# Reordering the vector engine's steps inside each attention unit of a hybrid encoder block: sums of q and the split of turned softmax weights first, scaling and block transposes of the next head behind them

## The chip, the cores and the metric

One Trainium2 chip, one core. The metric is device time in microseconds of one execution of the whole program (one encoder layer, batch 1, 256 positions, width 2048, everything float32 from and to HBM). The kernel before takes 915.23 us (median of three runs, 915.09 to 915.6).

## What is computed

One layer: RMSNorm, one input projection into q, k, v and u, windowed attention with ALiBi and a sink logit on q, k, v (12 query heads of 128, 4 key heads, so three query heads share a key head), a Fourier mix on u, an output projection with residual, then a convolutional gated feed-forward with residual, then a last RMSNorm. What the change touches is the attention:

```
scores = einsum('bnqkgd,bnskd->bnkgqs', qb, kb) * HEAD_DIM ** -0.5
scores = where(valid, scores + alibi, NEG_INF)
m = maximum(max(scores, axis=-1), sink_b)
p = exp(scores - m)
p = p / (sum(p, axis=-1) + exp(sink_b - m))
out = einsum('bnkgqs,bnskd->bnqkgd', p, vb)
...
x = x + concatenate([rmsnorm(out), fourier], -1) @ w_out
x = x + conv_ffn(rmsnorm(x)); return rmsnorm(x)
```

## The kernel before

Float32 accuracy is reached on TensorE with split operands: every operand is written as a high part `hi` (rounded by ScalarE, `nc.scalar.activation(hi, raw, AF.Copy)`, L185) and a low part `lo = raw - hi` (VectorE, L186), and a product is formed from hi x hi, lo x hi and hi x lo. So each weight tile that is streamed in (128 x 2048 floats, 1 MB) costs one long ScalarE instruction and one long VectorE instruction. In the profile PE is TensorE, DVE is VectorE, ACT is ScalarE, POOL is GpSimd and SP is the engine that issues most DMAs.

The first half of the program is a row of numbered **units**, one weight tile each. Units 4 to 7 make v, units 8 to 23 make the q and k heads in the order k0 q0 q1 q2, k1 q3 q4 q5, k2 q6 q7 q8, k3 q9 q10 q11, units 24 to 39 are the output projection. A unit is run by

```
def unit(i, work):
    run(before, i)
    work(*halves.pop(i))
    run(beside, i)
    step(i)
    run(behind, i)
```

`work` is the unit's matmuls (for a q or k head 32 of them, L395 and L397, about 5.25 us). `before` holds other matmuls that run first on TensorE; `beside` and `behind` hold the small steps of the other engines, and `step(i)` between them splits the weight tile of unit i + 2 (L185, L186) and then issues the load of the tile of unit i + 5 from SP. The order is written out by hand: each engine takes its instructions strictly in the order in which the program names them, and waits in place for whatever the next one needs.

A query head whose matmuls run in unit s goes through these steps afterwards:

- unit s + 1, `qk_out` (L637 ACT copies half of the PSUM result to `tmp`, L639 DVE adds the halves: the "sum of q") and `qk_parts` (L234 ACT, L235 DVE: the hi and lo of q, tile `qT`). A key head does the same with L639, L641, L654, L655.
- unit s + 2, `scores` (six matmuls, L665, in `before`, each lo part of q used by the third of each three), `scores_out` (DVE, L681 to L686) and, in `behind`, `exps` (ACT, L695 and L699).
- unit s + 3, `weigh` (DVE, L704 to L708: sum, reciprocal and scaling by it) and `turn` (L715: VectorE transposes blocks of 32 x 32 into the one buffer `tb`; L720: SP writes it to DRAM, tile `turn`).
- unit s + 4, `fetch` (L726: four DMAs from SP read the blocks back from DRAM in turned order into `td`, two buffers).
- unit s + 5, `turn_out` (L739 ACT, L740 DVE: hi and lo of the turned weights, tiles `pt`).
- unit s + 6, `values` (six matmuls, L768, in `before`; the second one already needs the lo part) and `values_out` (L492 and L234 on ACT, L235 on DVE, tile `cat`; a sum on POOL, L497).

The last head, 11, is transposed by TensorE instead (`turn_last`, `turn_last_out`, unit 27) and its values are formed in unit 28 with those of head 10.

Because every fourth unit is a key head, the duties of VectorE and ScalarE repeat with a period of four units. By what they hold, four kinds of unit are told apart below, named after an example in the middle:

- kind 18 (units 14, 18, 22): weigh, turn, sum and parts of a q, turn_out.
- kind 19 (15, 19, 23): sum and parts of a q, scores_out, values_out, turn_out.
- kind 20 (16, 20, 24): weigh, turn, sum and parts of a q, scores_out, values_out, turn_out.
- kind 21 (13, 17, 21, 25): weigh, turn, sum and parts of a k (in 25: none), scores_out, values_out; no turn_out.

All of them end with the split of a weight tile. The order in which a unit's small steps are queued is the order of the `at(beside, ...)` calls in the loop at L782 to L820, which is what the change edits. On DVE it is before: weigh, turn, sum of q, (k), parts, scores_out, values_out, turn_out, split. On SP a unit queues fetch, the write of turn, and, after the split has released its buffer, the load.

Of the kernel before, what the change touches and what calls it, by code (L numbers as in the profile page):

```python
# [96 lines left out]
def block_kernel(  # L97
# [42 lines left out]
    def bank(pool, name):  # L140
        return pool.tile([P, 512], F32, tag=pool.name, name=name)
# [63 lines left out]
    for n, size in enumerate(U_LOADS[1:], 1):  # L205
        k = sum(U_LOADS[:n])
# [18 lines left out]
    ps = bank(dn, "ps_warm")  # L225
# [68 lines left out]
    k = 0  # L294
# [119 lines left out]
    before, beside, behind = {}, {}, {}  # L414

    def at(when, i, f, *a):
        when.setdefault(i, []).append((f, a))
# [214 lines left out]
    qk_sb, st = {}, {}  # L632
    sq_a = ph.tile([P, S], F32, tag="sq", name="sq_a")

    def qk_out(kind, h, ps):
        tmp = ph.tile([P, S], F32, tag="tmp", name=f"tmp_{kind}{h}", bufs=2)
        nc.scalar.activation(tmp, ps[:, S : 2 * S], AF.Copy)  # L637
        add = ph.tile([P, S], F32, tag="add", name=f"add_{kind}{h}", bufs=2)
        nc.vector.tensor_tensor(add, ps[:, 0:S], tmp, ALU.add)  # L639
        if kind == "k":  # L640
            nc.vector.tensor_tensor(add, add, r1b, ALU.mult)  # L641
        st["add", kind, h] = add
# [139 lines left out]
    for i in range(N_QK, N_OUT + 8):  # L782
        heads = {i - s: h for (kind, h), s in slot_of.items() if kind == "q"}
        new = [kh for kh, s in slot_of.items() if i - s == 1]
        if i - 9 in range(NG):
            at(before, i, fourier_channels, i - 9)
        valued = [h for d, h in heads.items() if d == (5 if h == NH - 1 else 6)]
        for h in valued:
            at(before, i, values, h, mm if i < N_OUT else dn)
        turned = {d: h for d, h in heads.items() if h < NH - 1}  # L790
        last = {d: h for d, h in heads.items() if h == NH - 1}
        if 4 in last:
            at(before, i, turn_last, last[4])
        if i == 15:
            at(before, i, total, sq_f, "f")
        if 2 in heads:
            at(before, i, scores, heads[2])
        if 4 in turned:
            at(beside, i, fetch, turned[4])
        if 3 in heads:  # L800
            at(beside, i, weigh, heads[3])
        if 3 in turned:
            at(beside, i, turn, turned[3])

        for kind, h in new:
            if kind == "q":
                at(beside, i, lambda k=kind, h=h: qk_out(k, h, st.pop(("ps", k, h))))
        if 4 in last:
            at(beside, i, turn_last_out, last[4])
        for kind, h in new:  # L810
            if kind == "k":
                at(beside, i, lambda k=kind, h=h: qk_out(k, h, st.pop(("ps", k, h))))
            at(beside, i, qk_parts, kind, h)
        if 2 in heads:
            at(beside, i, scores_out, heads[2])
            at(behind, i, exps, heads[2])
        for h in valued:
            at(beside, i, values_out, h)
        if 5 in turned:
            at(beside, i, turn_out, turned[5])  # L820

    fourier_channels_steps()
    for n, (kind, h) in enumerate(QK_ORDER):
# [57 lines left out]
    for n, (c, kq) in enumerate(OUT_ORDER):  # L881
        i = N_OUT + n
# [14 lines left out]
        if kq >= 2:  # L897
            part = "a" if kq == 2 else "f"
            ps = ps_a[c] if kq < 3 else ps_a[c, "f"]
            last = c in added  # L900
# [306 lines left out]
    for q in range(2):  # L1207
        kind, j = items[q]
        ps = bank(mm, f"ps_{kind}{j}")
# [16 lines left out]
    for n, it in enumerate(items):  # L1226
# [8 lines left out]
        if it[0] in ("gate", "val"):  # L1235
            kind, j = it
            ps = bank(mm, f"ps_{kind}{j}")
# [4 lines left out]
        if it[0] == "product":  # L1242
            kind, g, c, p = it
# [3 lines left out]
            for cc in (0, 1) if both else (c,):  # L1247
# [5 lines left out]
                ps = bank(mm, f"ps_{p}{g}{cc}")  # L1253
# [6 lines left out]
        else:  # L1260
            kind, g, c = it
            hi, lo = halves.pop(up_index[n])
            ps = [bank(mm, f"ps_l{g}{c}{b}") for b in range(2)]
# [10 lines left out]
    i = up_index[n]  # L1274
# [156 lines left out]
```

## Time and profile before

| what | value |
| --- | --- |
| median of 3 runs | 915.23 us |
| the profiled execution, its own time | 915.61 us |
| its span, first to last instruction | 913.8 us, so 1.8 us lie around it |
| mean granted TensorE clock | 0.992 |
| PE busy over the span | 896.7 us (98%) |
| DVE busy | 753.5 us (82%) |
| ACT busy | 546.0 us (60%) |
| POOL busy | 53.2 us (6%) |
| DMA moved | 220.62 MB, 241 GB/s |

The profile's columns: a row of the timeline is start, duration (us), engine, line, operation, tiles (written <- read), shapes, count, and in brackets the idle time of the engine before it with what ended it. A row of the waits is who waited for whom: total us, times, longest. A row of the windows is the stretch, its length, then busy time and (x instructions) of PE, PE's weight loads, DVE, ACT and POOL, then the granted TensorE clock (1.00 is full speed), the DMA share and GB/s. Attention's units 12 to 28 lie between 75 and 190 us of the span.

### The profile page before, as it was taken

The numbers are of one execution on the slowest core, as the hardware profiler recorded it, in microseconds if no ns is written. First come the engines' busy times: TensorE is split into PE (matmuls) and PEld (weight loads), VectorE is DVE, ScalarE is ACT, GpSimd is POOL, SyncE is SP. The second block draws the span as 40 slices with busy tenths as digits, with TensorE's granted clock in tenths as the row PEclk, the third lists the DMA queues.
The fourth block names the chain that finished last, engine by engine and source line by source line (L and its number), as shares of the span: only waits on it lengthen the run. The fifth ranks groups of instructions, "written<-read, shape, count | busy, mean of one in ns | idle before, by whom it ended". The sixth has DMA issues, their size and how long they took to land.

```text
span 913.8 us, 12775 instructions
## 1 busy us (share of the span) xinstructions
PE 896.7 (98%) x5020; PEld 808.9 (89%) x5020; DVE 753.5 (82%) x905; ACT 546.0 (60%) x661; POOL 53.2 (6%) x65
## 2 busy tenths in 40 slices
PE   9999898999999999999999999999999999999996
PEld 7899787988899999999999999999999999999885
DVE  7668888867668787889888898878988789988996
ACT  7756556655545656556655575555665555656544
POOL 0001101010000000000000000000000000000004
PEclk9999899999999999999999999999999999999999
DMA  9964566655559687686988779896887987789752
GB/s 362 333 231 173 185 204 195 229 199 180 207 180 305 232 265 230 209 264 206 300 243 274 241 282 248 258 320 209 284 262 237 312 276 237 242 259 272 221 198 92
DMA packets 40827, 220.62 MB, mean 241 GB/s; under 512 B 4512, under 2 KB 10528, under 8 KB 16448
## 3 DMA queue, kind: packets, MB, share of 16 engines
q1 hardware_dynamic: 36512, 190.06, 56.2%
q0 software_dynamic: 4112, 29.49, 17.4%
q8 instruction: 39, 0.64, 0.3%
q10 hardware_dynamic: 144, 0.26, 0.1%
q14 instruction: 20, 0.16, 0.0%
HBM read 214.81 MB, written 4.98 MB: 241 GB/s over the span
## 4 chain that ended last, share of the span: by engine, by line
PE 83%; DVE 8%; ACT 4%; issue 2%; DMA 1%; POOL 1%; ACTq 0%; POOLq 0%; DVEq 0%
PE ps_val L395 16%; PE ps_gate L395 16%; PE ps_gate L397 8%; PE ps_val L397 8%; DVE parts L186 4%; PE ps_P L1148 3%; PE ps_P L1149 3%; PE ps_P L1150 3%; PE ps_N L1148 2%; PE ps_N L1150 2%; PE ps_N L1149 2%; PE ps_u L289 2%; PE ps_a L379 2%; PE ps_a L378 2%; PE ps_a L380 2%
## 5 line engine op out<-in xcount | busy, mean ns | idle before, releaser
L186 DVE TENSOR_TENSOR parts<-raw,parts 128x2048 fp32r<-128x2048 f32 (+1 forms) x129 | 293.2, 2273 | 49.9 <-ACT parts L185 47.1
L185 ACT ACTIVATE parts<-raw 128x2048 fp32r<-128x2048 f32 (+1 forms) x129 | 245.5, 1903 | 43.2 <-PE ps_a L380 12.4
L395 PE MATMUL ps_val<-hU,parts 128*128 128x512 f32 x688 | 227.7, 382 | 0.0
L395 PE MATMUL ps_gate<-hU,parts 128*128 128x512 f32 x688 | 227.3, 382 | 0.0
L397 PE MATMUL ps_val<-hU,parts 128*128 128x256 f32 x688 | 187.7, 273 | 0.0
L397 PE MATMUL ps_gate<-hU,parts 128*128 128x256 f32 x688 | 187.0, 273 | 0.0
L395 PEld LDWEIGHTS ps_val<-hU,parts 128*128 128x128 f32 x688 | 130.6, 190 | 17.7
L395 PEld LDWEIGHTS ps_gate<-hU,parts 128*128 128x128 f32 x688 | 130.5, 190 | 17.7
L397 PEld LDWEIGHTS ps_val<-hU,parts 128*128 128x128 f32 x688 | 132.2, 192 | 0.7
L397 PEld LDWEIGHTS ps_gate<-hU,parts 128*128 128x128 f32 x688 | 131.9, 192 | 0.9
L926 ACT ACTIVATE ft_g<-ps_gate 128x256 f32<-128x256 f32 x43 | 16.5, 383 | 112.9 <-PE ps_gate L397 110.2
L395 PE MATMUL ps_q<-hT,parts 128*128 128x512 f32 x192 | 64.5, 393 | 0.0
L926 ACT ACTIVATE ft_v<-ps_val 128x256 f32<-128x256 f32 x43 | 16.4, 382 | 73.4 <-PE ps_val L397 73.4
L1148 PE MATMUL ps_P<-parts_P,op_P 128*128 128x512 f32 x144 | 54.7, 380 | 0.0
L1149 PE MATMUL ps_P<-parts_P,op_P 128*128 128x512 f32 x144 | 54.7, 380 | 0.0
L1150 PE MATMUL ps_P<-parts_P,op_P 128*128 128x512 f32 x144 | 54.7, 380 | 0.0
L397 PE MATMUL ps_q<-hT,parts 128*128 128x256 f32 x192 | 51.5, 278 | 0.0
L1034 DVE TENSOR_TENSOR parts_N<-sumw,parts_N 128x2048 fp32r<-128x2048 f32 x18 | 41.3, 2292 | 9.9 <-ACT parts_N L1033 9.9
L395 PEld LDWEIGHTS ps_q<-hT,parts 128*128 128x128 f32 x192 | 37.5, 196 | 5.1
L1148 PE MATMUL ps_N<-parts_N,op_N 128*128 128x512 f32 x108 | 41.1, 380 | 0.0
L1150 PE MATMUL ps_N<-parts_N,op_N 128*128 128x512 f32 x108 | 41.0, 380 | 0.0
L1149 PE MATMUL ps_N<-parts_N,op_N 128*128 128x512 f32 x108 | 41.0, 380 | 0.0
(347 smaller groups left out, 1558.8 us busy)
## 6 DMA issues: line engine op xcount, KB each, us to landing
raw<-in_w_up SPq DMA_DIRECT2D x86, 1024.0 KB, 6.4
raw<-in_w_in SPq DMA_DIRECT2D x20, 1024.0 KB, 5.2
sumw<-in_w_down POOLq DMA_DIRECT2D x18, 1024.0 KB, 8.6
raw<-in_w_out SPq DMA_DIRECT2D x16, 1024.0 KB, 4.9
raw<-in_w_down_late SPq DMA_DIRECT2D x4, 1024.0 KB, 6.0
u_raw<-in_u_in SPq DMA_DIRECT2D x4, 768.0 KB, 10.7
raw<-in_w_down_last SPq DMA_DIRECT2D x4, 768.0 KB, 4.7
turn<-tb SPq DMA_DIRECT2D x11, 256.0 KB, 4.4
```

The lines of the kernel that those rows point to most:

```text
L185: nc.scalar.activation(hi, raw, AF.Copy)
L186: nc.vector.tensor_tensor(lo, raw, f32(hi), ALU.subtract)
L289: nc.tensor.matmul(ps_u[b], block(hk(k), part, b, True), in_turn(w), start=k == 0 and n == 0, stop=k == NK - 1 and n == 2,)
L378: nc.tensor.matmul(ps, ah, wh, start=first and q == q0, stop=False)
L379: nc.tensor.matmul(ps, al, wh, start=False, stop=False)
L395: nc.tensor.matmul(ps, hi[:, s], in_turn(h), start=k == 0, stop=False)
L397: nc.tensor.matmul(ps[:, 0:S], lo[:, s], in_turn(h)[:, 0:P], start=False, stop=k == NK - 1)
L926: nc.scalar.activation(tmp, ps[:, S : 2 * S], AF.Copy)
L1034: nc.vector.tensor_tensor(lo, src, f32(hi), ALU.subtract)
L1148: nc.tensor.matmul(ps, o[:, 0, p, :], wh, start=first and p == 0, stop=False)
L1149: nc.tensor.matmul(ps, o[:, 1, p, :], wh, start=False, stop=False)
L1150: nc.tensor.matmul(ps, o[:, 0, p, :], wl, start=False, stop=end)
```

## The change

Inside each unit's `beside` list, the sum of q (`qk_out` of a query head) and `turn_out` are moved to the front, with `turn_last_out` behind them, ahead of `weigh` and `turn`. `turn_out` was the last step of the list. Nothing is added or taken away; every instruction and DMA is the same. On DVE the order is after it: sum of q, turn_out, (turn_last_out), weigh, turn, (k), parts, scores_out, values_out, split; on ACT the copy for the sum of q, then the hi part of turn_out, then the parts of q or k, the two steps of values_out, the split, the exponentials. On SP the order stays fetch, write of turn, load.

```diff
@@ -797,16 +797,18 @@
             at(before, i, scores, heads[2])
         if 4 in turned:
             at(beside, i, fetch, turned[4])
+
+        for kind, h in new:
+            if kind == "q":
+                at(beside, i, lambda k=kind, h=h: qk_out(k, h, st.pop(("ps", k, h))))
+        if 5 in turned:
+            at(beside, i, turn_out, turned[5])
+        if 4 in last:
+            at(beside, i, turn_last_out, last[4])
         if 3 in heads:
             at(beside, i, weigh, heads[3])
         if 3 in turned:
             at(beside, i, turn, turned[3])
-
-        for kind, h in new:
-            if kind == "q":
-                at(beside, i, lambda k=kind, h=h: qk_out(k, h, st.pop(("ps", k, h))))
-        if 4 in last:
-            at(beside, i, turn_last_out, last[4])
         for kind, h in new:
             if kind == "k":
                 at(beside, i, lambda k=kind, h=h: qk_out(k, h, st.pop(("ps", k, h))))
@@ -816,8 +818,6 @@
             at(behind, i, exps, heads[2])
         for h in valued:
             at(beside, i, values_out, h)
-        if 5 in turned:
-            at(beside, i, turn_out, turned[5])
```

## The prediction

> **What bounds the kernel now.** I read TensorE's waits first, because it is the engine with the least idle time; then stretches of the span with the granted clock; then the timelines of each engine around the waits.
>
> ```profile
> PE ps_o L768 <- ACT pt L739: 6.1, 3, 3.9
> PE ps_o L768 <- DVE pt L740: 1.7, 3, 1.0
> ```
>
> These are six waits of the attention values on the turned weights `pt`, 7.8 us together. The stretches show what else they cost:
>
> ```profile
> 95.64:101.30 5.66, 5.51 (x21) 5.04 (x22) 4.05 (x7) 3.23 (x6) 0.00 (x0) 0.50 0.46 129
> 124.30:152.25 27.95, 26.05 (x165) 23.62 (x164) 23.33 (x51) 17.56 (x35) 2.47 (x3) 1.00 0.61 198
> 156.02:159.40 3.38, 3.38 (x13) 2.92 (x12) 2.88 (x4) 1.05 (x4) 0.26 (x1) 0.51 0.52 126
> 188.00:908.00 720.00, 717.95 (x4021) 649.97 (x4020) 608.11 (x624) 422.88 (x445) 38.54 (x41) 1.00 0.76 243
> ```
>
> After two of the waits TensorE ran at half clock, 5.66 and 3.38 us long, which costs half of each: 2.8 and 1.7. So at most 7.8 + 4.5 = 12.3 us are to be had. The last row says that from 188 us on TensorE hardly stands: what attention gains stays. The second row holds units 19 to 22: TensorE's own work is 26.05 us for four units. The waits stand here:
>
> ```profile
> 95.64 0.58 PE L768 MATMUL ps_o<-pt,v_hi 128*128 128x256 f32 x1 [3.91 <-ACT pt L739]
> ```
> ```profile
> 153.91 0.38 PE L768 MATMUL ps_o<-pt,v_hi 128*128 128x256 f32 x1 [1.69 <-ACT pt L739]
> 154.64 0.38 PE L768 MATMUL ps_o<-pt,v_hi 128*128 128x256 f32 x1 [0.35 <-DVE pt L740]
> ...
> 155.30 0.93 PE L665 MATMUL ps_s<-kT,qT 128*128 128x256 f32 x6
> 156.02 0.64 PE L395 MATMUL ps_q<-hT,parts 128*128 128x512 f32 x1
> ```
>
> The first is unit 15, the others unit 23, the latest of the six. Why is `pt` late? VectorE, from the start of unit 18 to that of unit 22:
>
> ```profile
> 121.64 0.15 DVE L704 TENSOR_TENSOR sm<-sm,ex 128x2 f32<-128x2 f32 x1
> ...
> 122.68 0.71 DVE L715 STREAM_TRANSPOSE tb<-sc 128x512 f32<-128x512 f32 x1
> 123.31 0.38 DVE L639 TENSOR_TENSOR add_q<-ps_q,tmp_q 128x256 f32<-128x256 f32 x1
> 124.26 0.42 DVE L235 SCALAR_TENSOR_TENSOR qT<-add_q,qT 128x256 fp32r<-128x256 f32 x1 [0.56 <-ACT qT L234]
> 124.77 0.69 DVE L740 TENSOR_TENSOR pt<-td,pt 128x512 fp32r<-128x512 f32 x1
> 126.58 2.29 DVE L186 TENSOR_TENSOR parts<-raw,parts 128x2048 fp32r<-128x2048 f32 x1 [1.12 <-DMA raw<-in_w_in]
> 128.78 0.42 DVE L639 TENSOR_TENSOR add_q<-ps_q,tmp_q 128x256 f32<-128x256 f32 x1
> 129.80 0.47 DVE L235 SCALAR_TENSOR_TENSOR qT<-add_q,qT 128x256 fp32r<-128x256 f32 x1 [0.59 <-ACT qT L234]
> 130.18 0.41 DVE L681 CUSTOM_DVE_ANT_0 sc<-ps_s,rel 128x256 f32<-128x256 f32 x1
> ...
> 131.32 0.48 DVE L235 SCALAR_TENSOR_TENSOR cat<-ps_o,vec,cat 128x256 fp32r<-128x256 f32 x1
> 131.71 0.68 DVE L740 TENSOR_TENSOR pt<-td,pt 128x512 fp32r<-128x512 f32 x1
> 132.75 2.29 DVE L186 TENSOR_TENSOR parts<-raw,parts 128x2048 fp32r<-128x2048 f32 x1 [0.36 <-ACT parts L185]
> 134.96 0.15 DVE L704 TENSOR_TENSOR sm<-sm,ex 128x2 f32<-128x2 f32 x1
> ```
> ```profile
> 142.76 0.15 DVE L704 TENSOR_TENSOR sm<-sm,ex 128x2 f32<-128x2 f32 x1
> ```
> ```profile
> 150.82 0.15 DVE L704 TENSOR_TENSOR sm<-sm,ex 128x2 f32<-128x2 f32 x1
> ```
>
> From start to start, kind 18 takes 7.14 us, kind 19 6.18, kind 20 7.80, kind 21 8.06: 29.2 for four units, against TensorE's 26.05. VectorE sets the pace of attention, and TensorE waits where it hands over `pt`. So the gain is what VectorE's units lose in length up to the last hand-over, plus how much earlier in its unit that hand-over comes. ScalarE is in the same chain: its split can't start before its own copy for `pt`, which stood behind the late sum of q:
>
> ```profile
> 124.11 0.62 ACT L739 ACTIVATE pt<-td 128x512 fp32r<-128x512 f32 x1
> 124.63 1.91 ACT L185 ACTIVATE parts<-raw 128x2048 fp32r<-128x2048 f32 x1
> ```
>
> That copy and split end at 126.54, where VectorE's wait of 1.12 us before its split ends; the name of a DMA in that row is not what it waited for.
>
> **The change, part by part.** No instruction is added. Three things happen.
>
> *Sum of q and its parts.* With the sum first, ScalarE's hi part of q is made while VectorE does `pt`, scaling and transposes, so the waits of 0.56 and 0.59 us before `qT` go. The sum now needs ScalarE's copy at once, where 1.67 us of scaling and transposes (122.68 - 121.64 and 123.31 - 122.68) covered it. I cost that at nothing, since TensorE has finished the earlier unit while it stands waiting for VectorE; if TensorE were the later one, each unit would pay the rest of that copy, at most those 1.67 us, and by then TensorE would be the bound.
>
> *Kind 18.* What is left is its work: scaling 1.04, transposes 0.63, sum 0.38, parts 0.42, `pt` 0.69, split 2.20 (128.78 - 126.58), together 5.36 us. ScalarE does `pt` (0.52 until the next start), q's hi part and the split (1.91) in some 2.9 us, before VectorE is there at 3.16. So all three waits go: 7.14 - 5.36 = 1.78 us saved.
>
> *The new wait.* `turn_out` at the head of the queue needs `td`, which comes over DRAM:
>
> ```profile
> 121.75 0.35 SPq L177 DMA_DIRECT2D raw<-in_w_in  x1
> 122.15 1.85 SPq L726 DMA_DIRECT2D td<-turn  x4
> 124.10 0.38 SPq L720 DMA_DIRECT2D turn<-tb  x1
> ```
> ```profile
> L726 SPq DMA_DIRECT2D td<-turn x4: 423/427/432, 122.2 to 123.6; - x4
> ...
> DMA to landing us min/median/max: 4.5/4.8/5.1
> ```
> ```profile
> L720 SPq DMA_DIRECT2D turn<-tb x11: 331/338/379, 77.6 to 174.2; - x11
> ...
> DMA to landing us min/median/max: 2.9/4.4/5.3
> ```
>
> The last of these four fetches is issued at 123.6 and lands about 4.5 later, 6.4 us after the unit's start. Behind the waiting `pt` stand, on ScalarE, q's hi part, the values' steps and the split; on VectorE everything of the unit. TensorE waits for q's parts among them.
>
> *Kind 19.* Kind 18 now lasts 5.36, so its `td` is there 1.1 us into kind 19; with ScalarE's copy `pt` starts on VectorE at about 1.85 instead of 0.42. Then 0.69 + 0.38 + 1.14 + 0.39 brings it to 4.45, ScalarE's split ends at about 4.65, and 2.21 of split make 6.87: 0.7 longer than the 6.18 now.
>
> *Kind 20.* Its work is 1.04 + 0.63 + 0.42 + 0.38 + 1.14 + 0.39 + 0.69 + 2.21 = 6.90, so 0.9 would be saved. But its `td` is fetched only when the write of kind 18 has landed: transposes end 2.8 us into kind 18 (0.38 + 0.69 + 1.04 + 0.71), 4.4 for the write, so 1.9 us into kind 19. One fetch before had to wait in this way:
>
> ```profile
> 178.88 1.86 SPq L726 DMA_DIRECT2D td<-turn  x4
> ```
> ```profile
> 185.64 0.63 ACT L739 ACTIVATE pt<-td 128x512 fp32r<-128x512 f32 x1 [1.94 <-DMA td<-turn]
> ```
>
> 6.76 us from first issue to use: by that, 1.8 us into kind 20, `pt` at 2.4, VectorE stands 2.0 and the unit costs 1.1 more than now. The other end: 1.43 from first to last issue and 2.9, the shortest landing, so 6.2 into kind 19: no wait, 0.9 saved. I take 3.7 for the landing, between the shortest and the usual, since a fetch issued 1.9 us later has less of the 1 MB load ahead of it: 7.0, a stand of about 0.4, and 0.5 saved. The Trainium skill, "DMA: Bandwidth & Descriptors", section "Queues, rings and completion order", says that on each DMA engine descriptors are consumed in ring order; by that a late fetch ends no later behind the load than a punctual one, the wait goes wholly, and the gain is 0.8 larger, 909.1. The one late fetch of this trace does not bear that out: 6.76.
>
> *Kind 21* has neither step: 8.06 as now. Per four units 1.78 - 0.7 + 0.5 = 1.6 us, ends 0 and 2.0. Before unit 14 the sum of q in unit 12 loses a wait as well:
>
> ```profile
> 78.44 0.46 DVE L235 SCALAR_TENSOR_TENSOR qT<-add_q,qT 128x256 fp32r<-128x256 f32 x1 [0.60 <-ACT qT L234]
> ```
>
> *Hand-over in unit 22 to 23.* Now q11's first matmul starts 156.02 - 150.82 = 5.2 us after VectorE's start of unit 22. After: 0.38 + 0.69 + 1.04 + 0.63 + 0.42 = 3.2 until q's lo part, which the scores need, and then four of the six scores matmuls (0.72 for six): 3.7. That is 1.5 earlier; the wait for `pt` gives way to one for `qT`, which is later than before in its unit.
>
> **Sum:** 0.6 + 2 x 1.6 + 1.5 = 5.3 us (ends 2.1 and 6.1). The half clock after unit 23 I leave: TensorE, 3.1 us quicker per four units, will still stand there about as long. SP's loads wait for the split, not for `turn`, and shift with it; POOL keeps its order. From the execution's own 915.61 that gives 910.3; it lay 0.4 above the median, so 909.9.
>
> On the clock: a wait of 1.69 us with 0.35 behind it was enough for the half clock of 156.02 to 159.40. The Trainium skill, "TensorE: Matmul & The Clock Gate", section "HAM oscillation — how this bites in real kernels", has the rule that idle gaps over about 3.4 us are to be avoided. By that rule no wait left would cost clock and the time would be 908.2; the trace shows a shorter one doing it.
>
> **Rivals.** *Nearly all of it (0.12).* The fetches land early, VectorE gets ahead and unit 23 doesn't stand long enough to lose the clock. Unit 15 keeps 3.91 - 0.6 - 1.5 = 1.8; the rest, 12.3 - 1.8, is up to 10.5, or 7.7 with its 2.8 of half clock: about 906. For it: 2.9 as shortest landing. Against: it needs both kinds 19 and 20 free of stands, and kind 19's 6.4 shows in the rows. The two rules of the Trainium skill named above (the ring order of "DMA: Bandwidth & Descriptors", the gap length of "TensorE: Matmul & The Clock Gate") would both lead this way.
>
> *No difference (0.07).* The late fetch of 6.76 in each kind 20: two groups save nothing, 2.1 is left, and one more such stand near unit 26 to 28 takes 1.1: 914.2.
>
> *Slower (0.10).* The DRAM round trip takes over the pace, as `turn_out` holds up all that VectorE and ScalarE have behind it, the next head's transposes included, whose write and fetch then start later still. If `td` comes x later than I took in kinds 19 and 20, the gain is 5.3 - 4x: it turns at x = 1.3, and at 2.4 the gain is -4.3 and the time 919.5. For it: kind 19 is certain to stand, and ScalarE stands with it. Against: the landings quoted lie between 4.5 and 5.1, and the one late fetch gives x = 1.6 in kind 20 alone.
>
> **How the numbers follow.** My forecast has 0.71, with gains of 2.1 to 6.1, or up to 7.8 with the clock kept. Two tenths of a per cent, 1.8 us, is what a measurement can tell here. Faster: 0.71 + 0.12 = 0.83; same 0.07; slower 0.10. The range for 8 in 10 goes from 906.8, inside the first rival, to 914.0, just past the forecast's weak end; left out are the slower rival and the extremes.
>
> **What would show it.** Right: no wait of `ps_o` on `pt` longer than 1.3 us; waits of `ps_s` on `qT` instead; no wait of VectorE's `qT` on ScalarE in kinds 18 to 20; kind 18 about 5.4 us long, kind 19 about 6.9; ScalarE's `pt` waiting on `td` in kinds 19 and 20. Wrong: stands on `td` of over 2 us in each, four units as long as 29 us, or new waits of TensorE after 190 us.

## The result, and the profile after

The changed kernel takes 909.28 us (median; 908.96 to 909.62), the kernel before 915.38: a ratio of 0.9934, interval 0.9916 to 0.9951. The forecast was 909.9, range 906.8 to 914.0. Two later comparisons of the same kernel gave 910.07 and 910.10 (0.9947, 0.9932 to 0.9962, and 0.9947, 0.9934 to 0.9959), so its gain is 5 to 6 us. The profiled execution took 908.96 us, its span 907.2. Of all executions reported below one, of the variant in units 26 and 27, took 3110 us for an unknown reason; its ratio leaves that one out.

TensorE's waits in the changed kernel (total us, times, longest):

```profile
PE ps_o L768 <- DVE pt L740: 2.7, 4, 0.9
PE ps_s L665 <- DVE qT L235: 2.3, 3, 0.9
```

7.8 us of waits for `pt` have become 2.7, and three waits of the scores for q's lo part are new. The waits between 56 and 190 us show what was gained on VectorE and what it cost. First the kernel before, then the changed one:

```profile
DVE qT L235 <- ACT qT L234: 6.7, 12, 0.6
```
```profile
ACT pt L739 <- DMA td<-turn: 17.4, 8, 3.8
...
DVE pt L740 <- ACT pt L739: 8.3, 7, 2.1
...
DVE qT L235 <- ACT qT L234: 1.2, 2, 0.6
```

The twelve waits of `qT`, 6.7 us, are down to two, both ahead of unit 12. In their place ScalarE now waits eight times for the weights to come back from DRAM, and VectorE stands idle for 8.3 us behind it; such an idle wait is called a stand below. VectorE in units 18 and 19:

```profile
118.38 0.42 DVE L639 TENSOR_TENSOR add_q<-ps_q,tmp_q 128x256 f32<-128x256 f32 x1
118.71 0.68 DVE L740 TENSOR_TENSOR pt<-td,pt 128x512 fp32r<-128x512 f32 x1
...
120.36 0.71 DVE L715 STREAM_TRANSPOSE tb<-sc 128x512 f32<-128x512 f32 x1
120.99 0.38 DVE L235 SCALAR_TENSOR_TENSOR qT<-add_q,qT 128x256 fp32r<-128x256 f32 x1
121.30 2.28 DVE L186 TENSOR_TENSOR parts<-raw,parts 128x2048 fp32r<-128x2048 f32 x1
123.50 0.42 DVE L639 TENSOR_TENSOR add_q<-ps_q,tmp_q 128x256 f32<-128x256 f32 x1
125.47 0.69 DVE L740 TENSOR_TENSOR pt<-td,pt 128x512 fp32r<-128x512 f32 x1 [1.56 <-ACT pt L739]
126.08 0.47 DVE L235 SCALAR_TENSOR_TENSOR qT<-add_q,qT 128x256 fp32r<-128x256 f32 x1
...
128.31 2.29 DVE L186 TENSOR_TENSOR parts<-raw,parts 128x2048 fp32r<-128x2048 f32 x1 [0.24 <-ACT parts L185]
130.52 0.42 DVE L639 TENSOR_TENSOR add_q<-ps_q,tmp_q 128x256 f32<-128x256 f32 x1
```

Unit 18 has no wait left and is 5.1 us long (123.50 - 118.38), unit 19 stands 1.56 us at its second instruction and is 7.0. The DMA issues beside it, and the landings of the fetch for unit 20 (the late fetch) and of the load in front of it:

```profile
118.49 0.35 SPq L177 DMA_DIRECT2D raw<-in_w_in  x1
118.89 1.85 SPq L726 DMA_DIRECT2D td<-turn  x4
121.10 0.34 SPq L720 DMA_DIRECT2D turn<-tb  x1
123.60 0.35 SPq L177 DMA_DIRECT2D raw<-in_w_in  x1
125.31 1.75 SPq L726 DMA_DIRECT2D td<-turn  x4
```
```profile
L726 SPq DMA_DIRECT2D td<-turn x4: 318/426/436, 125.3 to 126.6; - x4
...
DMA to landing us min/median/max: 3.6/4.1/4.4
```
```profile
L177 SPq DMA_DIRECT2D raw<-in_w_in x1: 352/352/352, 123.6 to 123.6; - x1
...
DMA to landing us min/median/max: 5.9/5.9/5.9
```

The fetch for unit 20 waits for the write of unit 18 and goes out 1.8 us into unit 19, where the forecast had 1.9; its last part lands 3.6 us after 126.6, at 130.2, 0.7 behind the load (129.5).

TensorE where unit 22 hands over to unit 23:

```profile
145.90 0.38 PE L768 MATMUL ps_o<-pt,v_hi 128*128 128x256 f32 x1
147.03 0.38 PE L768 MATMUL ps_o<-pt,v_hi 128*128 128x256 f32 x1 [0.75 <-DVE pt L740]
...
147.69 0.39 PE L665 MATMUL ps_s<-kT,qT 128*128 128x256 f32 x2
149.00 0.71 PE L665 MATMUL ps_s<-kT,qT 128*128 128x256 f32 x4 [0.93 <-DVE qT L235]
149.55 0.38 PE L395 MATMUL ps_q<-hT,parts 128*128 128x512 f32 x1
```

The first two scores matmuls run, the other four wait for q's lo part. q11 starts 3.6 us after VectorE's start of unit 22 (145.96), 5.2 before. The stretch behind it, the rest of the program, and, for comparison, the same stretch in another profiled execution of the changed kernel:

```profile
149.50:156.20 6.70, 6.70 (x47) 6.28 (x47) 4.63 (x12) 3.61 (x6) 0.96 (x1) 1.00 0.94 304
188.00:902.00 714.00, 711.31 (x3987) 642.67 (x3985) 605.40 (x622) 419.98 (x441) 35.58 (x39) 1.00 0.76 244
```
```profile
149.65:153.06 3.41, 3.41 (x12) 3.05 (x13) 2.47 (x2) 0.00 (x0) 0.00 (x0) 0.50 0.94 298
```

In the first the clock stayed up, in the other it was halved for 3.41 us.

### The profile page after: what moved, and what is told of

Same layout as the page of the kernel before. It is cut to its first block, busy times and chain, and to the rows that moved or that the text cites. A ratio compares the mean times of both kernels' runs of the same rounds, so it can differ in the third digit from the quotient of the medians.

```text
span 907.2 us, 12781 instructions
## 1 busy us (share of the span) xinstructions
PE 893.2 (98%) x5020; PEld 804.0 (89%) x5020; DVE 753.1 (83%) x905; ACT 545.9 (60%) x661; POOL 54.3 (6%) x65
## 4 chain that ended last, share of the span: by engine, by line
PE 81%; DVE 8%; DMA 3%; issue 3%; ACT 3%; POOL 1%; SPq 1%; ACTq 0%; POOLq 0%; DVEq 0%
PE ps_val L395 17%; PE ps_gate L395 17%; PE ps_gate L397 8%; PE ps_val L397 8%; PE ps_P L1148 3%; PE ps_P L1150 3%; PE ps_P L1149 3%; PE ps_N L1148 2%; PE ps_N L1150 2%; PE ps_N L1149 2%; DVE parts L186 2%; PE ps_u L289 2%; DMA td<-turn 2%; PE ps_a L380 2%; PE ps_a L378 2%
## 5 line engine op out<-in xcount | busy, mean ns | idle before, releaser
L186 DVE TENSOR_TENSOR parts<-raw,parts 128x2048 fp32r<-128x2048 f32 (+1 forms) x129 | 293.1, 2272 | 43.4 <-ACT parts L185 42.7
L395 PE MATMUL ps_q<-hT,parts 128*128 128x512 f32 x192 | 62.2, 383 | 0.0
```

Source lines behind the costliest of these rows:

```text
L186: nc.vector.tensor_tensor(lo, raw, f32(hi), ALU.subtract)
L395: nc.tensor.matmul(ps, hi[:, s], in_turn(h), start=k == 0, stop=False)
```

## The experiments

All edits are against the changed kernel, in the same loop. Theory A: VectorE's unit length sets the pace, and the early sum of q shortens it by taking away waits for ScalarE; `turn_out` at the head gives an earlier hand-over and costs a stand on `td`. Theory B: forming `pt` at the head is what counts. Theory C: the stand on `td` is idle time off the path, which costs nothing. The unit lengths are from one end of a split on VectorE (L186, start + duration) to the next; the times of matmuls are starts; the profile's own start of unit 12 differs by up to 0.65 us between runs.

| kernel | kind 18 | kind 19 | kind 20 | kind 21 | four units | q11 starts | ratio to before (interval) | median us |
| --- | --- | --- | --- | --- | --- | --- | --- | --- |
| before | 7.15 | 6.18 | 7.80 | 8.06 | 29.2 | 156.02 | 1 | 915.1 to 915.4 |
| the change | 5.11 | 7.03 | 7.30 | 8.14 | 27.6 | 149.55 | 0.9934 (0.9916 to 0.9951) | 909.28 |
| sum first alone | 5.55 | 6.19 | 6.71 | 8.09 | 26.5 | 149.53 | 0.9918 (0.9903 to 0.9933) | 907.69 |
| turn_out first alone | 7.17 | 6.70 | 8.51 | 8.10 | 30.5 | 157.60 | 1.0033 (1.0020 to 1.0046) | 918.15 |
| order by kind | 5.18 | 6.16 | 7.17 | 8.09 | 26.6 | 146.39 | 0.9918 (0.9902 to 0.9935) | 907.22 |
| fetch behind turn | 5.11 | 8.18 | 7.19 | 8.13 | 28.6 | 151.71 | 0.9960 (0.9946 to 0.9974) | 911.89 |
| fetch before load | 5.11 | 5.66 | 9.38 | 8.10 | 28.2 | 149.70 | 0.9917 (0.9903 to 0.9932) | 907.88 |
| by kind, early fetch | 5.19 | 6.17 | 7.26 | 8.10 | 26.7 | 146.75 | 0.9900 (0.9885 to 0.9915) | 905.92 |

The units are 18 to 21 of one profiled execution each. The rows were measured in several comparisons, each beside the kernel before, so the ratios are safer to compare than the times.

**The sum of q alone at the head.**

```diff
-        if 5 in turned:
-            at(beside, i, turn_out, turned[5])
...
         for h in valued:
             at(beside, i, values_out, h)
+        if 5 in turned:
+            at(beside, i, turn_out, turned[5])
```

> Only the sum of q is moved to the front; turn_out stays last in its unit. Theory A (VectorE's unit length sets the pace; the early sum takes away its waits for ScalarE): kind 18 falls from 7.1 to about 5.5 us, kind 19 stays near 6.2 because no DRAM wait is added, kind 20 from 7.8 to about 6.9, so four units take about 26.7 us, less than the 27.6 with the whole change; the hand-over of pt is only 0.8 us earlier. Gain 0.6 + 2 x 2.5 + 0.8 = 6.4 us, time 908 to 910. Theory B (what counts is that pt is formed at the head of the unit): pt moves by the 0.6 us of one wait only, gain at most 2 us, time 913 or more.

907.69 us. VectorE in unit 18 and the start of unit 19:

```profile
118.61 0.42 DVE L639 TENSOR_TENSOR add_q<-ps_q,tmp_q 128x256 f32<-128x256 f32 x1
...
120.62 0.41 DVE L235 SCALAR_TENSOR_TENSOR qT<-add_q,qT 128x256 fp32r<-128x256 f32 x1
120.95 0.67 DVE L740 TENSOR_TENSOR pt<-td,pt 128x512 fp32r<-128x512 f32 x1
121.95 2.29 DVE L186 TENSOR_TENSOR parts<-raw,parts 128x2048 fp32r<-128x2048 f32 x1 [0.33 <-ACT parts L185]
124.16 0.42 DVE L639 TENSOR_TENSOR add_q<-ps_q,tmp_q 128x256 f32<-128x256 f32 x1
125.18 0.48 DVE L235 SCALAR_TENSOR_TENSOR qT<-add_q,qT 128x256 fp32r<-128x256 f32 x1 [0.60 <-ACT qT L234]
```

`pt` is last again, only 0.8 us earlier in the unit than before, and the gain is all there and more (a little under the 908 to 910 that A gave): the wait before the split is 0.33 instead of 1.12, that on `qT` in kind 18 is gone, and no unit up to 24 stands on `td`. Theory A held in the length of each of these units; B is out.

**turn_out alone at the head.**

```diff
-        for kind, h in new:
-            if kind == "q":
-                at(beside, i, lambda k=kind, h=h: qk_out(k, h, st.pop(("ps", k, h))))
         if 5 in turned:
             at(beside, i, turn_out, turned[5])
-        if 4 in last:
-            at(beside, i, turn_last_out, last[4])
...
             at(beside, i, turn, turned[3])
+        for kind, h in new:
+            if kind == "q":
+                at(beside, i, lambda k=kind, h=h: qk_out(k, h, st.pop(("ps", k, h))))
+        if 4 in last:
+            at(beside, i, turn_last_out, last[4])
```

> Only turn_out is moved to the front; the sum of q stays behind weigh and turn. Theory A: VectorE keeps its waits of 0.6 us for qT and 1.1 us before the split in kind 18 (7.1 to 7.3 us long), kind 20 gets the wait for td and becomes 8 us or more; four units take 29 to 30 us as before; only the hand-over is earlier, and that is lost again: 914 to 917. Theory B: nearly the whole gain, 909 to 911.

918.15 us: slower than before, past the upper end that A gave. TensorE's waits:

```profile
PE ps_s L665 <- ACT qT L234: 4.5, 3, 1.6
PE ps_o L768 <- DVE pt L740: 2.6, 4, 0.8
PE ps_o L768 <- ACT pt L739: 1.9, 4, 0.7
```

The waits for `pt` fell from 7.8 to 4.5 us and 4.5 us of waits for q's hi part came up in their place. VectorE kept its waits of 0.5 and 1.4 us in kind 18 (the second again bears a DMA's name) and got the stand on `td` in kinds 19 (below) and 20 (0.54 in unit 20):

```profile
125.61 0.42 DVE L235 SCALAR_TENSOR_TENSOR qT<-add_q,qT 128x256 fp32r<-128x256 f32 x1 [0.50 <-ACT qT L234]
127.42 2.29 DVE L186 TENSOR_TENSOR parts<-raw,parts 128x2048 fp32r<-128x2048 f32 x1 [1.38 <-DMA raw<-in_w_in]
130.08 0.69 DVE L740 TENSOR_TENSOR pt<-td,pt 128x512 fp32r<-128x512 f32 x1 [0.37 <-ACT pt L739]
```

**The order by kind of unit.**

```diff
...
+        steps = {
+            0: [sum_q, weigh_turn, out_turned, parts_qk, post_scores, post_values],
+            1: [sum_q, out_turned, weigh_turn, parts_qk, post_scores, post_values],
+            2: [sum_q, out_turned, parts_qk, weigh_turn, post_scores, post_values],
+            3: [sum_q, parts_qk, post_scores, post_values, out_turned, weigh_turn],
+        }
+        for put in steps[i % 4]:
+            put()
```

The names are the same steps as before, each put in a function, and the old lines are left out here; i % 4 is 0 for kind 20, 1 for 21, 2 for 18, 3 for 19.

> The order differs by kind of unit: kind 18 sum, turn_out, parts of q, scaling, transposes; kind 19 sum, parts, scores_out, values_out, and turn_out last; kind 20 sum, scaling, transposes, turn_out, parts, scores_out, values_out. Theory A: the stand on td in kind 19 (0.8 us there now) goes, four units take about 26.5 us and q's parts are handed over 1.7 us earlier in kind 18: 905.5 to 908. Theory B: pt is later than with the change in kinds 19 and 20, so the time is above the change's 909.3, 910 to 912.

907.22 us, 2.9 below the changed kernel measured beside it, and no better than the sum alone (907.69; both ratios are 0.9918). q11 starts 3.2 us earlier than with the change. Four units took 26.6 us, as A had it; the stand in kind 19 is gone in units 15 and 19 (6.14 and 6.16 us) but not in unit 23 (7.05). B is out here too.

**The changed kernel again.**

> The changed kernel itself, as a control for this call. 908.9 to 909.7. If the half clock after unit 23 comes back in this profile, the attention stage is longer by up to 1.7 us from there, of which most is waited for anyway, so about 0.6 us in all; if the clock stays up, the time is about 909.0.

910.07 us (909.45 to 911.62), somewhat above what was expected; the clock stayed up in this profile.

**A later fetch.**

```diff
-        if 4 in turned:
-            at(beside, i, fetch, turned[4])
...
         if 3 in turned:
             at(beside, i, turn, turned[3])
+        if 4 in turned:
+            at(beside, i, fetch, turned[4])
```

> The changed kernel with the four fetches queued on SP behind the unit's write of turn instead of ahead of it. In kind 18 they then go out about 2.8 us into the unit instead of 0.5, so td lands some 1.6 to 1.8 us later for kind 19; kind 19 fetches as before (it writes no turn). Theory A (the stand on td in kind 19 is on the path, each us of it costs a us): kinds 19 become 8.6 to 8.9 us long instead of 7.1, two of them count ahead of the last hand-over: 3 to 4 us slower than the changed kernel, 912.5 to 914. Theory C (the stand on td is idle time off the path, as TensorE is ahead): 909 to 910, as the changed kernel.

911.89 us, 1.8 above the 910.07 of the changed kernel, and so less than the 3 to 4 that A expected; the two ratios' intervals overlap. The place is as expected, VectorE in unit 19:

```profile
124.15 0.41 DVE L639 TENSOR_TENSOR add_q<-ps_q,tmp_q 128x256 f32<-128x256 f32 x1
127.25 0.69 DVE L740 TENSOR_TENSOR pt<-td,pt 128x512 fp32r<-128x512 f32 x1 [2.68 <-ACT pt L739]
```

The stand grew by 1.1 us, not 1.7, and in the units of kind 20 behind it (7.29, 7.19 and 7.18 against 7.82, 7.30 and 7.94) some came back. This profile also holds a half clock from 150.29 on, so its start of q11 is not the stand's doing alone.

**An earlier fetch.**

```diff
-        if 4 in turned:
-            at(beside, i, fetch, turned[4])
...
         for h in valued:
             at(beside, i, values_out, h)
+        if 3 in turned:
+            at(beside, i, fetch, turned[3])
```

> The changed kernel with the fetch of a head issued at the end of the unit that wrote its turn, ahead of the 1 MB load on SP instead of behind it. td of kind 19 then lands some 3 us into kind 18 and VectorE doesn't stand there. Theory A: kind 19 falls from 7.1 to 5.5 to 6 us, four units take about 26.3 us, close to TensorE's own 26.05; 2.5 to 3.5 us faster than the changed kernel, 906 to 907.5. Theory C: no change, 909 to 910. In kind 18 the load waits for the fetch and so for the write, up to 2 us; it is used three units later, so that costs nothing.

907.88 us, 2.2 below the same 910.07. Kind 19 is 5.66 us in all three of its units: the stand is gone. The late and the early fetch were measured side by side, 4.0 us apart, and their intervals (0.9946 to 0.9974 and 0.9902 to 0.9932) lie apart: the place of the fetch in the queue costs time, and C is out. One unit of kind 20 went the other way, and the DMA issues of unit 18 show why:

```profile
128.62 0.42 DVE L639 TENSOR_TENSOR add_q<-ps_q,tmp_q 128x256 f32<-128x256 f32 x1
131.41 0.69 DVE L740 TENSOR_TENSOR pt<-td,pt 128x512 fp32r<-128x512 f32 x1 [2.37 <-ACT pt L739]
```
```profile
120.56 0.34 SPq L720 DMA_DIRECT2D turn<-tb  x1
125.40 1.74 SPq L726 DMA_DIRECT2D td<-turn  x4
```

That is unit 20 at 9.38 us (units 16 and 24: 7.25 and 7.28). Its fetch could go out only when the write of unit 18 had landed, 4.8 us after 120.56. In units 14, 18 and 22 that write landed 0.6 or 0.7 us behind the load in front of it (96.4 behind 95.8, 125.4 behind 124.7, 151.9 behind 151.3), and in unit 18 this load had gone out late, at 119.38, because it stood behind a fetch that had itself waited for a write. So a load held up by the fetch can cost something after all; the expectation had it at nothing. The last of the four parts then took 3.9 us, where those for units 16 and 24 took 2.0 at most; that is not settled.

**By kind, with the early fetch.** Both edits above.

> The order by kind of unit together with the early fetch. Theory A: with the order by kind there is little stand on td left (four units 26.6 us), so the early fetch adds at most 1 us: 905.5 to 907.5. If it is worth 2 us or more, td was still what VectorE waited for.

905.92 us, and 905.61 in a second comparison (0.9896, 0.9881 to 0.9911): the lowest times of all, 4 to 4.5 us below the changed kernel. It is 1.3 us below the order by kind alone, more than the 1 us expected; but the intervals of the two overlap, and the four units are no shorter, so what the early fetch adds there is not shown.

**The old place of turn_out in units 26 and 27.**

```diff
-        if 5 in turned:
+        if 5 in turned and i < 26:
             at(beside, i, turn_out, turned[5])
...
+        if 5 in turned and i >= 26:
+            at(beside, i, turn_out, turned[5])
```

> The changed kernel, but in units 26 and 27 turn_out is last in its unit as before the change. Up to the first matmul of unit 24 the changed kernel and the one with only the sum moved stand alike (156.13 and 156.11 us); the latter is 1.2 us ahead from unit 27 on. If that is the stand on td in units 26 and 27, which holds back turn_last_out and the split: about 1.2 us faster than the changed kernel, 908 to 909. If it is the longer chain up to unit 25: no difference, 909 to 910.

911.63 us (0.9958, 0.9944 to 0.9972). No gain, so the stand in these two units is not shown to be what separates the changed kernel from the sum alone. Its profile had lost 2.9 us by unit 24 already (first matmul at 159.07 against 156.13), with a longer stand in unit 20 (8.34 us against 7.30) and a half clock from 150.2 on, so it is inconclusive on the question asked.

**The closer comparison.**

> The changed kernel once more, beside the next two, for a closer comparison: 909 to 910.5 by what was measured so far.

> Only the sum of q first, turn_out last. Theory A (the early sum makes the gain, turn_out at the head adds a stand on td that takes back more than the earlier hand-over gives): 1 to 2.5 us faster than the changed kernel, 907 to 909. If turn_out at the head is worth nothing either way: within 0.5 us of it.

> Order by kind of unit and early fetch, the best so far: 905.5 to 907, 3 us below the changed kernel.

The change 910.10 (0.9934 to 0.9959), the sum alone 907.29 (0.9905 to 0.9933), by kind with early fetch 905.61. So the other half of the change, `turn_out` at the head, costs 2.8 us over the sum alone (2.4 in the first comparison), though the two intervals all but touch. The profiled executions of these two kernels in the table show where most of it goes. Counted from the first matmul of unit 12 (74.61 and 74.98), the sum alone is only 0.4 us ahead at the first matmul of unit 24 (156.11 against 156.13), but 1.6 us ahead at the first matmul of the output projection in unit 27 (174.25 against 175.48), and it stays so. In between, VectorE's units 23 and 24 take 7.24 and 7.95 us with the change, 6.18 and 6.72 with the sum alone, and in unit 26 `pt` of the change comes late:

```profile
173.50 0.69 DVE L740 TENSOR_TENSOR pt<-td,pt 128x512 fp32r<-128x512 f32 x1 [0.99 <-ACT pt L739]
```

The values of unit 27 wait for it. What lies between this 1.6 and the 2.4 to 2.8 is not accounted for; the half clocks, which differ from execution to execution, may be part of it.

## Why the prediction was right, point by point

- **What bounds.** VectorE's pace at 29.2 us for four units against TensorE's 26.05 was the right reading: what shortened VectorE's units moved TensorE, and what lengthened them (turn_out alone, 30.5) made the kernel slower.
- **Sum of q.** The waits on `qT` went as forecast, and the price of nothing for its new place held: no wait of VectorE on the sum shows in units 18 to 20.
- **Kind 18**: 5.36 forecast, 5.11 measured in units 18 and 22, 5.98 in unit 14. **Kind 19**: 6.87 forecast, 7.03 in unit 19, where `pt` starts 1.97 us into the unit (forecast 1.85), but 6.22 and 7.24 in units 15 and 23. **Kind 21**: 8.06 and 8.14.
- **Kind 20**: 7.3 forecast, 7.30 in unit 20, but 7.82 and 7.94 in units 16 and 24. The value taken between the ends was right for one unit of three. Its landing of 3.7 was 3.6; in units 16 and 24 the unit was not shortened at all.
- **Four units**: in units 18 to 21 1.6 us were saved, forecast 1.6. In units 14 to 17 it was 1.8, but made up otherwise: kind 18 saved 2.0 instead of 1.8, kind 19 lost 0.1 instead of 0.7, and kind 20 saved nothing instead of 0.5. That these misses nearly cancel is luck. **Hand-over**: 3.7 forecast, 3.6 measured, and the wait on `qT` in place of that on `pt` came as said.
- **Sum**: 5.3 forecast for q11's start; 156.02 - 149.55 = 6.5 measured, of which 0.6 was there before unit 12 (its predecessor's split ends at 74.37 instead of 74.94) and so is no effect of the change. The other 5.9 are 0.9 from units 12 and 13 (0.6 forecast), 1.8 and 1.6 from the two groups of four, and 1.6 from the hand-over (1.5).
- **The clock**: left as it was in the sum. It stayed up in the profiled execution (unit 24 starts 8.1 us earlier) and was halved in another one of the same kernel. Up to unit 28 some is given back, mostly in units 26 and 27, where `pt` is late as shown above: 187.38 - 180.74 = 6.6, which is the whole difference of the two executions, 6.65. The earlier half clock, in units 15 and 16, was gone too. The sum had no term for it, and VectorE's units account for the gain up to q11 without one.
- **The rivals.** The slower one named its mechanism rightly, and it is at work: it takes back 0.1, 0.9 and 1.2 us in the three units of kind 19. It decided alone, where turn_out came without the sum.
- **What the prediction lacked.** It never asked what each moved step would do alone, and gave the hand-over 1.5 of 5.3 us. Apart, the sum makes the whole gain, and `turn_out` at the head takes back more in stands than its hand-over brings: 2.4 and 2.8 us in the two comparisons.

## What to carry to other kernels

When two in-order engines pass work back and forth, put first what the other engine needs to go on; put what waits for a DMA round trip behind work that is ready, even if its consumer is the engine that stands. Cost moved steps one by one: of two moves in one edit, one made the gain and the other took some of it back. An order for each kind of unit together with an earlier fetch gave the lowest ratios, 0.9900 and 0.9896, where the changed kernel had 0.9934 to 0.9947. But the order by kind alone was no better than moving the sum alone (0.9918 both), and the 1.7 us that both edits together gained over it in one comparison lie within overlapping intervals, so that the finer order pays is not shown.

## What the runs showed of the hardware

The half clock came after less than I had thought to see. In one execution of the changed kernel waits of 0.34, 0.76 and 0.93 us within 3.5 us were followed by a half clock from 149.65 to 153.06, and waits of 0.87 and 0.48 us by one from 95.04 to 98.45; in another execution 0.12, 0.75 and 0.93 us, and 0.88 and 0.48 us, were not. Six traces hold halved stretches, and within each trace their edges lie whole multiples of 3.41 us apart (before: 94.47, 101.30, 155.91 and 159.32). In the windows of 3.41 us that these edges mark, from 50 us on, the clock was halved after every window with TensorE busy for less than half of it (nine, 0.20 to 0.49) and after none with 0.68 or more; in between, 0.60 and 0.61 were followed by a halved window and 0.57 was not. These figures fit with waits costing clock only where enough of them fall into one window; where the windows lie in the execution that kept its clock, its trace does not show. The Trainium skill, "TensorE: Matmul & The Clock Gate", section "What's actually happening", says that activity is judged in a free-running window of 3413 ns; the stretches of 3.41 us, and their coming and going between executions of the same kernel, agree with that. The same page's rule of gaps over about 3.4 us, which the prediction weighed, is not what these runs show: in those two executions of the changed kernel no single wait inside attention was over 0.93 us.

The late fetch lands with the load in front of it: 130.2 against 129.5 in unit 19. The Trainium skill, "DMA: Bandwidth & Descriptors", section "Queues, rings and completion order", has descriptors consumed in ring order on each engine, and this agrees; the one late fetch of the trace before also landed behind its load, but by 2.2 us (185.5 against 183.3). The load itself took 5.9 and 6.5 us in units 19 and 23 (5.0 the median before), so the order alone did not make the late fetch punctual.
